# A decoder layer on one core: the first group of columns of the input projection, seven products of halves replaced by eight blocks summed in PSUM

## The chip, the cores and the metric

The kernel runs on one core of one Trainium2 chip. A core has a matrix engine (TensorE, in the profile PE for its matmuls and PEld for its weight loads), a vector engine (VectorE, DVE), a scalar engine (ScalarE, ACT), a general engine (GpSimd, POOL) and a queue that issues transfers (SyncE, SP). TensorE writes to PSUM, which has 8 banks of 512 numbers of 32 bits in each of 128 partitions; the other operands lie in SBUF. Each engine works through its own queue in order. The metric is the time of one execution on the device in microseconds (us); lower is better.

## The reference

The reference is one layer of a decoder on 2,048 tokens of 1,024 features, in 32-bit floats. Ahead of everything stands a normalised input and one wide projection:

```python
nx = rmsnorm(h, attn_norm_g[l])
proj = jnp.einsum('bsd,dp->bsp', nx, w_in[l])
gq, gk, gv, gr, glow, dq, dk_, dv_ = jnp.split(proj, split_at, axis=-1)
```

Then come two mixers side by side (a gated linear attention on gq, gk, gv, gr, glow and a dilated sliding-window attention on dq, dk, dv), an output projection, and an MLP with squared ReLU; a last normalisation ends it. The change touches only the start of the projection: the 512 columns of dv for the first 1,024 tokens.

## The kernel before, in words

**Precision.** TensorE multiplies in a reduced format, so each operand is split into a high and a low half (`split`: ACT copies the high half, L368; DVE subtracts it to get the low half, L369), and `mm3` issues three matmuls per product (L64, L65, L66).

**Seven products.** The projection is done for each group of columns and each half of the tokens. Within such a pair the tokens are cut in two (tiles 0 to 3 and 4 to 7 of 128 tokens each), the 1,024 features in two, and the columns in two, and the 2 x 2 blocks are multiplied by the scheme of Strassen and Winograd: seven products of halves instead of eight, numbered 1, 2, 5, 6, 3, 4, 7 in the order of `order`, with sums of token blocks (`first_half`, `sixth_sum`, `last_sums`) and of weight blocks (in `prep`) ahead, and sums of results (`rest` inside `product`) behind. A job is one (group, product). `prep(at)` splits the weights of a job into one of three buffers `combs` (L207 on ACT, L209 on DVE) and makes the sums of raw weights; `load_w` fetches a quarter of a group's weights (L190). `product(at, i)` issues the matmuls of tile i, 12 of 256 columns for a group 256 wide, and takes a PSUM bank for two tiles in the turn a, c, a, o; its `rest` moves the bank out (L325 to L342, ACT or DVE) and calls `finish`, which stores finished results (L277, L279 for dv). There are nine groups; dv is group 0, gr (2 x 264 columns) is group 1.

**Token parts.** `TF[j]` holds the split token operand of product j, high half and low half, each a slot of SBUF; `parts(j, i)` is tile i of it. For the first 1,024 tokens these parts are made inside group 0: `x_load` fetches a tile, `x_stat` squares and sums it (ACT L378, DVE L380, a power on POOL L381), `x_scale` scales it (DVE L385), `turned` transposes it on TensorE in 8 pieces into one bank c and one bank d (L393), `first_half` makes its parts, and `kept` copies tiles 0 to 3 back to SBUF for the later sums (ACT L404). 25 slots of one size hold all of this; a slot is given out at the first write, so product 7's high half gets the slot of tiles 6 and 7 (`xt`) when those have been read for the last time, and its low half takes one of the three weight buffers.

**Order.** All of group 0 of the first half stands in one section (from L496 on) where the order of TensorE, DVE, ACT and POOL is the order written in the program; only SP's is free. In the section the seven products are threaded through the arrival of the tiles: products 1 and 2 of tile 0, 1, 2, 3 between the transposes of tiles 0 to 5, then 5, 6 and 3, then 4 and 7. Everything behind the section is ordered by a planner that works with its own costs of instructions. The next jobs (group 1) follow in a loop in which job at is preceded by `prep(at + 2)`.

Of the kernel before, what the change touches and what calls it, by code (L numbers as in the profile page):

```python
# [38 lines left out]
def emit(tc, a, stop=99):  # L39
# [115 lines left out]


    misc = slot("misc")
    gB, gnB, w2b = misc[:, :D], misc[:, D:D + 512], misc[:17, D + 512:D + 768]
# [20 lines left out]
    TF = {j: [slot(f"tb{j}", FR) for _ in range(2 if j < 7 else 1)] for j in order}  # L179
    xt = slot("xt")  # L180
    TB = {j: [view(t, (4, 512)) for t in TF[j]] for j in order}
    xs = [t[:, D * q:D * q + D] for t in (xp, bp) for q in range(2)] + [c21[:, :D], last[:, :D]]
    xs += [xt[:, D * q:D * q + D] for q in range(2)]
# [12 lines left out]

    def prep(at, sums=True):

# [13 lines left out]
        if j == 2 and g:  # L212
            V.tensor_tensor(a21, a21, a22, op=OP.add)
        if j == 5 and sums:
            V.tensor_tensor(a21, a21, a11, op=OP.subtract)
            load_w(g + 1, 0, 0)
            V.tensor_tensor(a12, a12, a21, op=OP.subtract)
# [22 lines left out]
    def outputs(g):  # L240

        return (c11, (c12, c22)[g % 2], c21, (c22, c12)[g % 2])

# [38 lines left out]
    banks, held = [0], {}  # L282

    def product(at, i):

# [5 lines left out]
        if e == 0:  # L291
            held[j, i] = ps("acao"[banks[0] % 4])
            banks[0] += 1
        p = held[j, i - e]
# [72 lines left out]
    def split(hi, lo, src):  # L367
        A.activation(hi, src, AF.Copy)  # L368
        V.tensor_tensor(lo, src, hi.bitcast(F32), op=OP.subtract)  # L369
# [6 lines left out]
    def x_stat(t):  # L376
        ss = stat()
        A.activation(TF[4][0][:, :D], xs[t], AF.Square, accum_out=ss)  # L378
        r, X[t] = stat(), stat()
        V.tensor_scalar(r, ss, 1.0 / D, EPS, op0=OP.mult, op1=OP.add)  # L380
        G.tensor_tensor(X[t], r, mhalf, op=OP.pow)  # L381
# [24 lines left out]
    def first_half(t, pv):  # L406

        i = t % 4
        b11, b21 = [view(xs[i][:, 512 * q:], (4, 128)) for q in range(2)]
        if t < 4:  # L410
            split(*parts(1, i), pv[0])
            split(*parts(2, i), pv[1])
            return
        t1, t2 = [view(xs[t][:, 512 * q:], (4, 128)) for q in range(2)]
        V.tensor_tensor(t1, pv[0], b11, op=OP.subtract)
        V.tensor_tensor(t2, pv[1], t1, op=OP.subtract)
        split(*parts(5, i), t1)
        split(*parts(6, i), t2)
        split(*parts(3, i), pv[1])

    def sixth_sum(i):
        b21, t2 = [view(xs[k][:, 512:], (4, 128)) for k in (i, i + 4)]
        V.tensor_tensor(b21, b21, t2, op=OP.subtract)

    def sixth_part(i):
        split(*parts(4, i), view(xs[i][:, 512:], (4, 128)))

# [68 lines left out]
    with tc.manual_schedule(engines={nc.tensor.engine, nc.vector.engine, nc.scalar.engine, nc.gpsimd.engine}):  # L496
        x_load(0, xs[0])
        g1, one = c11[:1, :D], CX[:1, :128]
        A.dma_start(g1, a["attn_norm_g"])
# [3 lines left out]
        load_w(0, 0, 1)  # L503
        x_load(2, xs[2])
        x_load(3, xs[3])
        load_w(0, 1, 0)
        load_w(0, 1, 1)
# [10 lines left out]
        x_scale(0)  # L518
        prep(0)

        def turned(t):
            return transposed(xs[t], by=perm)

        x_stat(1)
        pv0 = turned(0)
        split(*parts(1, 0), pv0[0])
        x_scale(1)
        split(*parts(2, 0), pv0[1])
        rest = product(0, 0)
        prep(1)  # L530
        x_stat(2)
        rest()
        pv1 = turned(1)
        kept(0, pv0)
        x_scale(2)
        first_half(1, pv1)
        rest = product(1, 0)
        x_stat(3)
        pv2 = turned(2)
        rest()  # L540
        kept(1, pv1)
        a21, a22 = [raws[1][:, k, :, :256] for k in range(2)]
        V.tensor_tensor(a21, a21, a22, op=OP.add)
        x_scale(3)
        x_stat(4)
        first_half(2, pv2)
        rests = [product(at, 1) for at in (0, 1)]
        pv3 = turned(3)
        for rest in rests:
            rest()  # L550
        kept(2, pv2)
        x_scale(4)
        x_stat(5)
        first_half(3, pv3)
        rests = [product(at, 2) for at in (0, 1)]
        pv4 = turned(4)
        for rest in rests:
            rest()
        kept(3, pv3)
        x_scale(5)  # L560
        prep(2, sums=False)
        x_stat(6)
        first_half(4, pv4)
        for at in (0, 1):
            product(at, 3)()
        pv = turned(5)
        (a11, a12), (a21, a22) = [[raws[n][:, k, :, :256] for k in range(2)] for n in range(2)]
        V.tensor_tensor(a21, a21, a11, op=OP.subtract)
        load_w(1, 0, 0)
        V.tensor_tensor(a12, a12, a21, op=OP.subtract)  # L570
        prep(3)
        prep(4)
        x_stat(7)
        x_scale(6)
        product(2, 0)()
        product(3, 0)()
        first_half(5, pv)
        pv = turned(6)
        product(4, 0)()
        x_scale(7)  # L580
        product(2, 1)()
        first_half(6, pv)
        product(3, 1)()
        pv = turned(7)
        product(4, 1)()
        first_half(7, pv)
        for at in (2, 3, 4):
            product(at, 2)()
        TF[7].append(combs[2])
        TB[7].append(view(TF[7][1], (4, 512)))  # L590
        rests = [product(2, 3)]
        combs[2] = slot("wcomb", FR)
        prep(5)
        sixth_sum(0)
        sixth_sum(1)
        sixth_part(0)
        rests += [product(at, 3) for at in (3, 4)]
        sixth_part(1)
        sixth_sum(2)
        sixth_sum(3)  # L600
        sixth_part(2)
        rests[0]()
        sixth_part(3)
        rests[1]()
        third = rests[2]
        rests = [product(5, i) for i in range(4)]
        prep(6)
        for i in (2, 3, 0):
            last_sums(i)
        for i in range(4):  # L610
            if i == 1:
                last_sums(1)
            if i % 2:
                rests[i]()
            split(*parts(7, i), view(xs[i], (4, 128)))
            if i == 1:
                third()
        rests = [product(6, i) for i in range(4)]
        prep(7)
        for rest in rests:  # L620
            rest()
        prep(8)
    other, back = second_half(), []
    for at in range(7, len(jobs)):
# [905 lines left out]
```

## Time and profile before

| | |
|---|---|
| median of 3 runs | 2313.16 us (2312.07 to 2315.47) |
| the profiled execution's own time | 2312.57 us |
| its span, first to last instruction | 2310.8 us |
| mean granted TensorE clock | 0.995 |
| instructions | 34,890 |
| first matmul of a projection block | at 10.19 us |
| last matmul of group 0 of the first half | at 73.12 us |

Profile lines show a start in us from the span's beginning, a duration in us, the engine, the line of the kernel, the operation, what it writes and reads, and shapes; in brackets the idle time of the engine just before and what ended it. Matmuls overlap one another in the pipeline, so their cost is the distance from start to start and not the duration shown. In stretches of the span the columns are the stretch, its length, and for each engine the busy time with the number of instructions, then the granted TensorE clock as a share of full speed, the busy share of the DMA engines and what they moved in GB/s. A line can be that of a helper: `split` is L368 and L369 whoever calls it.

### The profile page before, as it was taken

The numbers are of one execution on the slowest core, as the hardware profiler recorded it, in microseconds if no ns is written. First come the engines' busy times: TensorE is split into PE (matmuls) and PEld (weight loads), VectorE is DVE, ScalarE is ACT, GpSimd is POOL, SyncE is SP. The second block draws the span as 40 slices with busy tenths as digits, with TensorE's granted clock in tenths as the row PEclk, the third lists the DMA queues.
The fourth block names the chain that finished last, engine by engine and source line by source line (L and its number), as shares of the span: only waits on it lengthen the run. The fifth ranks groups of instructions, "written<-read, shape, count | busy, mean of one in ns | idle before, by whom it ended". The sixth has DMA issues, their size and how long they took to land.

```text
span 2310.8 us, 34890 instructions
## 1 busy us (share of the span) xinstructions
PE 2282.6 (99%) x12652; PEld 1975.6 (85%) x12652; DVE 1550.3 (67%) x2863; ACT 1179.3 (51%) x2368; POOL 307.7 (13%) x394
## 2 busy tenths in 40 slices
PE   8999999999999999999999999999999999999998
PEld 7977998799999998888888888888888888888887
DVE  8887778766667676346877788777755346447444
ACT  5574546435877873235555566555543323225224
POOL 1120002025385672000000000000000100000002
PEclk9999999999999999999999999999999999999999
DMA  4457854786668864678644447444486477447553
GB/s 165 144 183 230 250 161 125 215 254 229 209 203 249 253 218 143 210 244 279 208 153 151 151 163 265 151 151 150 150 278 238 155 280 251 148 166 279 188 170 109
DMA packets 341805, 457.59 MB, mean 198 GB/s; under 512 B 18118, under 2 KB 214231, under 8 KB 336257
## 3 DMA queue, kind: packets, MB, share of 16 engines
q1 hardware_dynamic: 336878, 446.71, 59.3%
q10 hardware_dynamic: 4754, 8.66, 1.0%
q8 instruction: 99, 1.62, 0.3%
q14 instruction: 74, 0.60, 0.1%
HBM read 292.99 MB, written 167.02 MB: 199 GB/s over the span
## 4 chain that ended last, share of the span: by engine, by line
PE 51%; ACT 1%; DMA 0%; DVE 0%; issue 0%; DVEq 0%; ACTq 0%
PE ps_c L64 6%; PE ps_c L65 6%; PE ps_c L66 6%; PE ps_a L65 4%; PE ps_a L66 4%; PE ps_d L65 4%; PE ps_d L64 4%; PE ps_a L64 4%; PE ps_d L66 4%; PE ps_o L65 2%; PE ps_o L66 2%; PE ps_o L64 2%; DMA w1raw<-w_ff 0%; ACT scr L1355 0%; DVE hb L369 0%; ACT hb L368 0%
## 5 line engine op out<-in xcount | busy, mean ns | idle before, releaser
L369 DVE TENSOR_TENSOR ca<-ra,ca 128x1024 fp32r<-128x1024 f32 x112 | 138.0, 1233 | 161.6 <-ACT ca L368 161.6
L368 ACT ACTIVATE ca<-ra 128x1024 fp32r<-128x1024 f32 x112 | 118.0, 1053 | 221.3 <-PE ps_c L66 184.3
L368 ACT ACTIVATE w1comb<-w1raw 128x512 fp32r<-128x512 f32 x224 | 140.0, 627 | 153.7 <-PE ps_c L66 55.7
L1357 POOL TENSOR_TENSOR suma<-suma,gs 128x512 f32<-128x512 f32 x16 | 23.4, 1475 | 1393.7 <-ACT scr L1355 1393.7
L369 DVE TENSOR_TENSOR w1comb<-w1raw,w1comb 128x512 fp32r<-128x512 f32 x224 | 153.9, 689 | 51.8 <-ACT w1comb L368 51.7
L785 PE MATMUL ps_a<-v,pt 128*128 128x65 f32 x1200 | 178.2, 252 | 2.5 <-ACT pt L773 1.8
L785 PEld LDWEIGHTS ps_a<-v,pt 128*128 128x128 f32 x1200 | 175.1, 195 | 3.5 <-ACT pt L773 2.1
L757 ACT ACTIVATE pe<-pe,O 128x256 f32<-128x256 f32 (+1 forms) x384 | 156.6, 453 | 39.4 <-DVE O L756 36.1
L766 PE MATMUL ps_d<-ident,pe 128*128 128x128 f32 x600 | 159.9, 279 | 0.0
L756 DVE CUSTOM_DVE_ANT_0 pe<-ps_c,nb 128x256 f32<-128x256 f32 (+1 forms) x384 | 126.9, 361 | 39.6 <-PE ps_d L766 18.4
L207 ACT ACTIVATE wcomb<-wraw 128x512 fp32r<-128x512 f32 (+2 forms) x126 | 97.2, 773 | 88.7 <-PE ps_o L65 22.6
L368 ACT ACTIVATE cb<-rb 128x1024 fp32r<-128x1024 f32 x56 | 59.4, 1060 | 159.3 <-PE ps_o L65 98.8
L66 PE MATMUL ps_c<-cb,ca 128*128 128x512 f32 x336 | 130.7, 389 | 0.0
L66 PE MATMUL ps_c<-hb,w1comb 128*128 128x512 f32 x336 | 130.7, 389 | 0.0
L65 PE MATMUL ps_c<-cb,ca 128*128 128x512 f32 x336 | 130.7, 389 | 0.0
L64 PE MATMUL ps_c<-hb,w1comb 128*128 128x512 f32 x336 | 130.7, 389 | 0.0
L65 PE MATMUL ps_c<-hb,w1comb 128*128 128x512 f32 x336 | 130.7, 389 | 0.0
L64 PE MATMUL ps_c<-cb,ca 128*128 128x512 f32 x336 | 130.7, 389 | 0.0
L766 PEld LDWEIGHTS ps_d<-ident,pe 128*128 128x128 f32 x600 | 110.1, 187 | 0.1
L369 DVE TENSOR_TENSOR cb<-rb,cb 128x1024 fp32r<-128x1024 f32 x56 | 68.3, 1222 | 62.0 <-ACT cb L368 62.0
L1219 ACT ACTIVATE acc<-acc 128x512 f32<-128x512 f32 x128 | 79.6, 631 | 51.5 <-DVE acc L1239 35.8
L64 PE MATMUL ps_a<-wo,mT 128*128 128x512 f32 x256 | 101.3, 396 | 0.0
(419 smaller groups left out, 7038.9 us busy)
## 6 DMA issues: line engine op xcount, KB each, us to landing
ra<-actD SPq DMA_DIRECT2D x56, 1024.0 KB, 6.9
actD<-acc SPq DMA_DIRECT2D x192, 256.0 KB, 2.3
rb<-w_ff SPq DMA_DIRECT2D x72, 512.0 KB, 4.8
w1raw<-w_ff SPq DMA_DIRECT2D x32, 1024.0 KB, 6.2
k<-kD SPq DMA_DIRECT2D x16, 1024.0 KB, 7.9
rb<-hTD SPq DMA_DIRECT2D x13, 1024.0 KB, 7.1
wraw<-w_in SPq DMA_DIRECT2D x48, 256.0 KB, 3.7
cmb<-boD SPq DMA_DIRECT2D x16, 528.0 KB, 7.0
```

The lines of the kernel that those rows point to most:

```text
L64: T.matmul(out, sh, mh, start=first, stop=False)
L65: T.matmul(out, sl, mh, start=False, stop=False)
L66: T.matmul(out, sh, ml, start=False, stop=last)
L207: A.activation(hi, src, AF.Copy, scale=sc)
L368: A.activation(hi, src, AF.Copy)
L369: V.tensor_tensor(lo, src, hi.bitcast(F32), op=OP.subtract)
L756: V.tensor_tensor_reduce(p, s, bias, scale=1.0, scalar=BIG, op0=OP.add, op1=OP.min, accum_out=nm)
L757: A.activation(p, p, AF.Exp, bias=nm, scale=-1.0)
L766: T.transpose(pb[:, i * 128:i * 128 + 128], src, ident)
L785: T.matmul(self.b.opsum[:, n % 4], self.pt[:, i * 128:i * 128 + 128], self.b.v[:, blk, cols], start=first, stop=last)
L1219: A.activation(v, v, AF.Relu)
L1357: G.tensor_tensor(C[0], C[0], gF[:, :512], op=OP.mult)
```

## The change

Group 0 of the first half is no longer computed by seven products but block by block: for each half of the columns n, each half of the features k and each tile t, `block(n, k, t)` multiplies the tile's own split block by the weights' own split block, and the two values of k are summed in PSUM (32 blocks of 12 matmuls for 28). The weights need four plain splits (`prep_block`, into the three `combs` and the low half's slot of product 7, which is now given out at the start) and no sums; `taken(n, t)` copies a finished bank of two tiles out on ACT and stores it. The results of group 0 get their own places, the fourth of them CX. `first_half` of tiles 4 to 7 now makes the parts of the tile's own two blocks (kept for the time being in the places of products 4 and 3); the sums of tokens for products 5, 6, 4 and 7 are made in the same section, as are their parts, but later (`sum_parts`, `sixth_sum`, `last_sums`), since only group 1 reads them. The last tile is transposed when 14 of the 32 blocks have been issued. The third weight load moves ahead of the load of tile 3, the four loads of group 1's weights are issued together, and the first turn of the PSUM banks is c instead of a.

```diff
--- before.py
+++ after.py
     combs = [slot("wcomb", FR) for _ in range(3)]
     TF = {j: [slot(f"tb{j}", FR) for _ in range(2 if j < 7 else 1)] for j in order}
     xt = slot("xt")
+    TF[7].append(slot("wcomb", FR))
     TB = {j: [view(t, (4, 512)) for t in TF[j]] for j in order}
-    xs = [t[:, D * q:D * q + D] for t in (xp, bp) for q in range(2)] + [c21[:, :D], last[:, :D]]
+    xs = [t[:, D * q:D * q + D] for t in (xp, bp) for q in range(2)] + [c22[:, :D], last[:, :D]]
     xs += [xt[:, D * q:D * q + D] for q in range(2)]
...
@@ -239,6 +241,8 @@
 
     def outputs(g):
 
+        if g == 0:
+            return c11, c12, c21, CX
         return (c11, (c12, c22)[g % 2], c21, (c22, c12)[g % 2])
 
     def finish(g, n, k, i):
@@ -281,6 +285,36 @@
 
     banks, held = [0], {}
 
+    def bank():
+        banks[0] += 1
+        return ps("acao"[banks[0] % 4])
+
+    first_w = [[combs[1], TF[7][1]], [combs[0], combs[2]]]
+
+    def prep_block(n, k):
+
+        w = view(first_w[n][k], (2, 4, 256))
+        split(w[:, 0], w[:, 1], raws[n][:, k, :, :256])
+
+    def block(n, k, t):
+
+        i, e = t % 4, t % 2
+        if k == e == 0:
+            held["first", n, t] = bank()
+        q = held["first", n, t - e][:, 256 * e:256 * e + 256]
+        B = TB[((1, 2), (4, 3))[t // 4][k]]
+        W = view(first_w[n][k], (2, 4, 256))
+        tk = slice(i * 128, i * 128 + 128)
+        for c in range(4):
+            mm3(q, B[0][:, c, tk], B[1][:, c, tk], W[:, 0, c], W[:, 1, c], k == c == 0, k == 1 and c == 3)
+
+    def taken(n, t):
+
+        i = t % 4
+        A.activation(outputs(0)[2 * n + t // 4][:, 256 * i:256 * i + 512], held["first", n, t], AF.Copy)
+        for m in (i, i + 1):
+            finish(0, n, t // 4, m)
+
...
     def product(at, i):
 
 
@@ -289,8 +323,7 @@
         two = w == 256
         e = i % 2 if two else 0
         if e == 0:
-            held[j, i] = ps("acao"[banks[0] % 4])
-            banks[0] += 1
+            held[j, i] = bank()
...
     def x_stat(t):
         ss = stat()
-        A.activation(TF[4][0][:, :D], xs[t], AF.Square, accum_out=ss)
+        A.activation(CX[:, :D], xs[t], AF.Square, accum_out=ss)
         r, X[t] = stat(), stat()
         V.tensor_scalar(r, ss, 1.0 / D, EPS, op0=OP.mult, op1=OP.add)
         G.tensor_tensor(X[t], r, mhalf, op=OP.pow)
...
     def first_half(t, pv):
 
         i = t % 4
-        b11, b21 = [view(xs[i][:, 512 * q:], (4, 128)) for q in range(2)]
         if t < 4:
             split(*parts(1, i), pv[0])
             split(*parts(2, i), pv[1])
             return
         t1, t2 = [view(xs[t][:, 512 * q:], (4, 128)) for q in range(2)]
-        V.tensor_tensor(t1, pv[0], b11, op=OP.subtract)
+        split(*parts(4, i), pv[0])
+        split(*parts(3, i), pv[1])
+        V.tensor_tensor(t1, pv[0], view(xs[i], (4, 128)), op=OP.subtract)
         V.tensor_tensor(t2, pv[1], t1, op=OP.subtract)
-        split(*parts(5, i), t1)
-        split(*parts(6, i), t2)
-        split(*parts(3, i), pv[1])
+
+    def sum_parts(i):
+        for q in range(2):
+            split(*parts(5 + q, i), view(xs[i + 4][:, 512 * q:], (4, 128)))
 
     def sixth_sum(i):
         b21, t2 = [view(xs[k][:, 512:], (4, 128)) for k in (i, i + 4)]
         V.tensor_tensor(b21, b21, t2, op=OP.subtract)
-
-    def sixth_part(i):
-        split(*parts(4, i), view(xs[i][:, 512:], (4, 128)))
 
     def last_sums(i):
         b11, t2 = view(xs[i], (4, 128)), view(xs[i + 4][:, 512:], (4, 128))
...
         x_load(0, xs[0])
-        g1, one = c11[:1, :D], CX[:1, :128]
+        g1, one = c11[:1, :D], c12[:1, :128]
         A.dma_start(g1, a["attn_norm_g"])
         V.memset(one, 1.0)
         load_w(0, 0, 0)
         x_load(1, xs[1])
         load_w(0, 0, 1)
         x_load(2, xs[2])
+        load_w(0, 1, 0)
         x_load(3, xs[3])
-        load_w(0, 1, 0)
         load_w(0, 1, 1)
         for t in range(4, 8):
             x_load(t, xs[t])
@@ -516,110 +548,98 @@
             T.matmul(p, one, g1[:, 512 * q:512 * q + 512], start=True, stop=True)
             V.tensor_copy(gB[:, 512 * q:512 * q + 512], p)
         x_scale(0)
-        prep(0)
+        prep_block(0, 0)
 
         def turned(t):
             return transposed(xs[t], by=perm)
 
+        def both(n, t):
+            for k in range(2):
+                block(n, k, t)
+
         x_stat(1)
-        pv0 = turned(0)
-        split(*parts(1, 0), pv0[0])
+        pv = turned(0)
+        split(*parts(1, 0), pv[0])
         x_scale(1)
-        split(*parts(2, 0), pv0[1])
-        rest = product(0, 0)
-        prep(1)
+        split(*parts(2, 0), pv[1])
+        block(0, 0, 0)
+        prep_block(0, 1)
         x_stat(2)
-        rest()
-        pv1 = turned(1)
-        kept(0, pv0)
+        prep_block(1, 0)
+        kept(0, pv)
+        pv = turned(1)
+        block(0, 1, 0)
         x_scale(2)
-        first_half(1, pv1)
-        rest = product(1, 0)
+        first_half(1, pv)
+        block(1, 0, 0)
         x_stat(3)
-        pv2 = turned(2)
-        rest()
-        kept(1, pv1)
-        a21, a22 = [raws[1][:, k, :, :256] for k in range(2)]
-        V.tensor_tensor(a21, a21, a22, op=OP.add)
+        kept(1, pv)
+        pv = turned(2)
+        both(0, 1)
         x_scale(3)
+        first_half(2, pv)
+        prep_block(1, 1)
         x_stat(4)
-        first_half(2, pv2)
-        rests = [product(at, 1) for at in (0, 1)]
-        pv3 = turned(3)
-        for rest in rests:
-            rest()
-        kept(2, pv2)
+        kept(2, pv)
+        pv = turned(3)
+        block(1, 1, 0)
+        taken(0, 0)
         x_scale(4)
+        first_half(3, pv)
+        both(1, 1)
         x_stat(5)
-        first_half(3, pv3)
-        rests = [product(at, 2) for at in (0, 1)]
-        pv4 = turned(4)
-        for rest in rests:
-            rest()
-        kept(3, pv3)
+        kept(3, pv)
+        for n in range(2):
+            for k in range(2):
+                load_w(1, n, k)
+        pv = turned(4)
+        both(0, 2)
         x_scale(5)
-        prep(2, sums=False)
         x_stat(6)
-        first_half(4, pv4)
-        for at in (0, 1):
-            product(at, 3)()
+        first_half(4, pv)
+        taken(1, 0)
         pv = turned(5)
-        (a11, a12), (a21, a22) = [[raws[n][:, k, :, :256] for k in range(2)] for n in range(2)]
-        V.tensor_tensor(a21, a21, a11, op=OP.subtract)
-        load_w(1, 0, 0)
-        V.tensor_tensor(a12, a12, a21, op=OP.subtract)
-        prep(3)
-        prep(4)
+        both(0, 3)
+        x_scale(6)
         x_stat(7)
-        x_scale(6)
-        product(2, 0)()
-        product(3, 0)()
         first_half(5, pv)
         pv = turned(6)
-        product(4, 0)()
+        both(0, 4)
         x_scale(7)
-        product(2, 1)()
+        taken(0, 2)
         first_half(6, pv)
-        product(3, 1)()
         pv = turned(7)
-        product(4, 1)()
+        sum_parts(0)
+        both(0, 5)
         first_half(7, pv)
-        for at in (2, 3, 4):
-            product(at, 2)()
-        TF[7].append(combs[2])
-        TB[7].append(view(TF[7][1], (4, 512)))
-        rests = [product(2, 3)]
-        combs[2] = slot("wcomb", FR)
-        prep(5)
-        sixth_sum(0)
-        sixth_sum(1)
-        sixth_part(0)
-        rests += [product(at, 3) for at in (3, 4)]
-        sixth_part(1)
-        sixth_sum(2)
-        sixth_sum(3)
-        sixth_part(2)
-        rests[0]()
-        sixth_part(3)
-        rests[1]()
-        third = rests[2]
-        rests = [product(5, i) for i in range(4)]
-        prep(6)
-        for i in (2, 3, 0):
+        both(0, 6)
+        sum_parts(1)
+        taken(0, 4)
+        sum_parts(2)
+        sum_parts(3)
+        both(0, 7)
+        for i in (2, 3, 1, 0):
+            sixth_sum(i)
             last_sums(i)
-        for i in range(4):
-            if i == 1:
-                last_sums(1)
-            if i % 2:
-                rests[i]()
+        taken(0, 6)
+        both(1, 4)
+        prep(7)
+        both(1, 5)
+        for i in range(2):
+            split(*parts(4, i), view(xs[i][:, 512:], (4, 128)))
             split(*parts(7, i), view(xs[i], (4, 128)))
-            if i == 1:
-                third()
-        rests = [product(6, i) for i in range(4)]
-        prep(7)
-        for rest in rests:
-            rest()
+        taken(1, 4)
+        both(1, 6)
+        split(*parts(4, 2), view(xs[2][:, 512:], (4, 128)))
+        split(*parts(7, 2), view(xs[2], (4, 128)))
+        both(1, 7)
+        taken(1, 6)
+        split(*parts(4, 3), view(xs[3][:, 512:], (4, 128)))
+        split(*parts(7, 3), view(xs[3], (4, 128)))
+        both(1, 2)
+        both(1, 3)
         prep(8)
+        taken(1, 2)
```

More of the change, by code (lines that the diff above doesn't have):

```diff
@@ L195, in comb, with prep @@
         return [t[:, q, :, :w] for q in range(2)]
-    def prep(at, sums=True):
+    def prep(at):
         if at >= len(jobs):
@@ L213, in prep @@
             V.tensor_tensor(a21, a21, a22, op=OP.add)
-        if j == 5 and sums:
+        if j == 5:
             V.tensor_tensor(a21, a21, a11, op=OP.subtract)
```

## The prediction

> **What bounds the kernel now.** I read the page first: the busy shares and the slices.
>
> ```profile
> PE 2282.6 (99%) x12652; PEld 1975.6 (85%) x12652; DVE 1550.3 (67%) x2863; ACT 1179.3 (51%) x2368; POOL 307.7 (13%) x394
> ...
> PE   8999999999999999999999999999999999999998
> ...
> PEclk9999999999999999999999999999999999999999
> ```
>
> TensorE is busy for 99% of the span. So work taken off another engine is worth something only where TensorE stands still, and work added to TensorE costs its full price where it does not. Where it stands still is seen in stretches of the span (busy time and instruction count for PE, PEld, DVE, ACT, POOL, then granted clock, DMA share, GB/s).
>
> ```profile
> 15.00:73.00 58.00, 49.79 (x374) 48.28 (x373) 52.63 (x74) 32.54 (x55) 4.62 (x5) 0.91 0.38 121
> 73.00:115.00 42.00, 42.00 (x348) 42.00 (x347) 36.46 (x57) 26.36 (x63) 7.21 (x8) 1.00 0.49 139
> 115.00:825.00 710.00, 707.80 (x5071) 648.97 (x5069) 520.08 (x1392) 435.68 (x1079) 222.34 (x294) 1.00 0.68 212
> 825.00:900.00 75.00, 70.55 (x536) 66.24 (x535) 62.09 (x179) 49.48 (x133) 47.30 (x61) 0.95 0.65 209
> 900.00:2250.00 1350.00, 1348.99 (x6067) 1119.29 (x6067) 843.52 (x1116) 599.52 (x955) 11.53 (x8) 1.00 0.59 198
> ```
>
> The first row is the stage that the change rewrites. TensorE idles 8.2 us there and its clock is 0.91; DVE, busy 52.6 of 58.0 us, is the fuller engine. From 73 to 115 us TensorE has no gap, and in the 2,135 us from 115 to 2250 it idles 7.7 us, 4.5 of them in one stretch. So whatever TensorE gains before 73 us moves everything behind it forward. TensorE's waits in the stage name the stalls (total, times, longest):
>
> ```profile
> PE ps_c L64 <- ACT wcomb L207: 2.6, 1, 2.6
> PE ps_a L64 <- ACT tb L368: 2.6, 2, 2.4
> PE ps_c L393 <- DVE xt L385: 1.5, 1, 1.5
> PE ps_c L66 <- DVE wcomb L209: 0.8, 1, 0.8
> ```
>
> These are split weights, split parts of tokens and a scaled tile: all come late out of the two queues that DVE and ACT work through in order. The timeline of TensorE gives the pace:
>
> ```profile
> 14.99 0.40 PE L64 MATMUL ps_c<-wcomb,tb 128*128 128x256 f32 x1
> ...
> 20.29 0.60 PE L393 MATMUL ps_c<-perm,bp 128*128 128x128 f32 x4
> ...
> 21.08 0.37 PE L64 MATMUL ps_a<-wcomb,tb 128*128 128x256 f32 x1
> ...
> 22.59 0.28 PE L64 MATMUL ps_o<-wcomb,tb 128*128 128x256 f32 x1
> ...
> 24.04 0.60 PE L393 MATMUL ps_c<-perm,acc 128*128 128x128 f32 x4
> ...
> 36.84 0.41 PE L65 MATMUL ps_c<-wcomb,tb 128*128 128x256 f32 x1
> 37.05 0.41 PE L66 MATMUL ps_c<-wcomb,tb 128*128 128x256 f32 x1
> ...
> 69.19 0.41 PE L64 MATMUL ps_a<-wcomb,tb 128*128 128x256 f32 x1
> 69.40 0.41 PE L65 MATMUL ps_a<-wcomb 128*128 128x256 f32 x1
> ...
> 71.69 0.29 PE L64 MATMUL ps_a<-wcomb,tb 128*128 128x264 f32 x1
> ...
> 73.24 0.28 PE L66 MATMUL ps_a<-wcomb,tb 128*128 128x264 f32 x1
> ```
>
> Twelve matmuls of 256 columns (one tile, one product) take 1.45 us, from 22.59 to 24.04. Eight transposes with twelve such matmuls take 2.30 (20.29 to 22.59), so the transposes are 0.85. After the two long stalls a matmul starts only every 0.21 us (36.84 to 37.05, 69.19 to 69.40), where it is 0.12 at full pace: a stall of 2.4 us costs about 1.4 us more behind it. The two matmuls of the second group that lie ahead of 73.24 are worth 0.25, so the second group in effect begins at 73.0.
>
> **The change, part by part.**
>
> *TensorE.* Group 0 of the first half had 7 products of 4 tiles, 28 blocks of 12 matmuls; it gets 2 x 2 x 8 = 32. That is 4 more: 4 x 1.45 = 5.8 us, with nothing beside it to hide under. The transposes stay 64.
>
> *DVE and ACT.* Costs per instruction, as start to start where the queue is full:
>
> ```profile
> 10.86 1.28 DVE L385 SCALAR_TENSOR_TENSOR xp<-xp,stats,misc 128x1024 f32<-128x1024 f32 x1
> 12.06 0.68 DVE L369 TENSOR_TENSOR tb<-ps_d,tb 128x512 fp32r<-128x512 f32 x1
> 12.67 1.22 DVE L209 TENSOR_TENSOR wcomb<-wraw,wcomb 128x1024 fp32r<-128x1024 f32 x1
> ...
> 33.95 1.22 DVE L209 TENSOR_TENSOR wcomb<-wraw,wcomb 128x1024 fp32r<-128x1024 f32 x1
> 35.20 1.22 DVE L219 TENSOR_TENSOR wraw<-wraw 128x1024 f32<-128x1024 f32 x1
> 36.34 1.22 DVE L209 TENSOR_TENSOR wcomb<-wraw,wcomb 128x1024 fp32r<-128x1024 f32 x1
> ```
>
> ```profile
> 10.89 1.05 ACT L207 ACTIVATE wcomb<-wraw 128x1024 fp32r<-128x1024 f32 x1
> 11.84 1.05 ACT L378 ACTIVATE tb<-bp 128x1024 fp32r<-128x1024 f32 x1
> ...
> 12.87 0.59 ACT L404 ACTIVATE xp<-ps_c 128x512 f32<-128x512 f32 x1
> 13.35 0.59 ACT L404 ACTIVATE xp<-ps_d 128x512 f32<-128x512 f32 x1
> ...
> 20.71 0.60 ACT L404 ACTIVATE bp<-ps_c 128x512 f32<-128x512 f32 x1 [0.30 <-DVE tb L369]
> ```
>
> On DVE 1024 elements take 1.15 (33.95 to 36.34, two of them with the small gaps between 2.39, so 1.2 at the most), a scaling 1.2 and 512 elements 0.61; on ACT 0.95 and 0.48. DVE loses 3 of 7 weight splits and 4 sums of raw weights (7 x 1.15 = 8.1) and the 14 additions of group 0's evictions (14 x 0.61 = 8.5): 16.6 us of its 52.6. ACT loses 3 weight splits (2.9) and has 8 evictions for 6 (+1.0). The 28 splits of token parts, 16 sums of tokens, 8 scalings and 8 squares stay. DVE comes to about 36 us and TensorE becomes the fuller engine.
>
> *The end of the stage.* Up to 15.0 us nothing differs: the first block needs what the first product needed. From there 31 blocks and 6 transposed tiles remain: 31 x 1.45 + 6 x 0.85 = 50.1, so group 0 ends at 65.1 if TensorE never waits, against 73.0: a gain of 7.9, which I round to 8.0. The same sum for the order before, 27 blocks and 6 tiles, is 44.3 of the 58.0 us: 13.7 us are idle time, slow pace and restarts. They go, and 5.8 come.
>
> *Does TensorE never wait?* I followed the three queues by hand in the new order, with these durations. The third weight block is split on ACT at 12.87 and ready from DVE at 15.1; TensorE wants it at 16.5. Tile 2 is scaled at 16.7, wanted at 17.95. Tile 1's parts: 17.9, wanted at 18.8. The fourth weight block: 22.2, wanted at 22.6. Tile 4 scaled: 24.2, wanted at 26.9. Later margins are 2.5 us and grow. The smallest is 0.4, so I allow 0 to 1.5 us of waiting and take 0, since even a late block delays by its lateness alone. ACT's copy of a tile out of PSUM waits for DVE's low halves out of the same bank (20.71, 0.30 behind L369); that is in these times.
>
> *The power on POOL* that stands ahead of every scaling:
>
> ```profile
> 14.02 0.55 POOL L381 TENSOR_TENSOR stats<-stats,pair 128x1 f32<-128x1 f32 x1 [3.20 <-DVE stats L380]
> 17.23 1.46 POOL L381 TENSOR_TENSOR stats<-stats,pair 128x1 f32<-128x1 f32 x1 [2.66 <-DVE stats L380]
> ```
>
> It takes 0.55 and once 1.46, beside a DVE sum of two SBUF operands. In the new order the third weight block's low half stands at that place, so tile 2's power gets 1.46 in my times; it uses 0.4 of a margin of 1.6. The Trainium skill (SBUF — State Buffer, "Who interferes with whom") says that a VectorE instruction with two SBUF inputs holds off a GpSimd one that reads SBUF until it is done; the 1.46 agrees, and by it every power could be 0.9 late, which the scalings' margins (1.2 at the least) cover.
>
> *Loads.* Two transfers swap places (the third weight block goes ahead of tile 3), and the second group's four weight loads are issued together.
>
> ```profile
> 4.55 1.33 SPq L190 DMA_DIRECT2D wraw<-w_in  x2
> ...
> wraw<-w_in SPq DMA_DIRECT2D x4, 512.0 KB, 6.4
> ```
>
> The two last weight loads were issued from 4.55 and took 6.4: 11 us, one place earlier now, for 12.87. Tile 3 comes a transfer later; its square stands at 15.8. Bound: 0 to 1 us; I take 0. The second group's loads wait on SP behind two stores of the first eviction (ACT, 22.9) and land before 35; the split that needs them stands at 48.
>
> *Behind the stage.* Splits for products 4 and 7 and the second weight split move behind block matmuls. The second split must wait for the last block (65.1) and is done at 67.4; the product that reads it starts after 48 matmuls, at 71. The token parts of product 7 still need the buffer of tiles 6 and 7, which made the 2.4 us stall, but over 10 us of block matmuls and the whole of products 1 to 4 of the second group now lie ahead of their use. Stores: 16 and 4, as before. The rotation of PSUM banks begins one place on for all later groups; the trace does not show its price. TensorE idles 2.2 us from 115 to 825, so it is bounded by -2.2 (all of that gone) and +2.2 (as much again), and I take 0.
>
> The sum against the profiled execution: 2312.6 - 8.0 = 2304.6. The median of the runs is 0.6 above that execution: 2305.
>
> **The rivals.**
>
> *The new order starves TensorE at the start* (chance 0.12). If one of the thin margins (0.4 to 1.4) breaks by a late load, TensorE stands 2.4 us and then runs at the slow pace: 2.4 + 1.4 = 3.8 of the 8.0 are lost, 2309. For it: four weight splits and four tiles still crowd into the first 25 us of DVE. Against: the walk above, and DMA needs to be over 1.8 us late. The Trainium skill (TensorE: Matmul & The Clock Gate, "Part 1") has the clock fall after an idle window of about 3.4 us; here 2.4 to 2.6 us were enough, so the trace decides. By the page alone this rival would cost 2.4, not 3.8.
>
> *The planner gives it back* (0.14). Only this stage has its order written out; everything behind it is ordered by the planner, which now starts from another time and another bank. TensorE's 7.7 us of idle time from 115 to 2250 (and the slow clock of 0.95 in the one bad stretch, 3.7 us) show how little it loses today; a second stretch like the one from 825 to 900 would cost 4.5 + 3.7 = 8.2, and the time would be 2313. For it: nothing holds the old order. Against: the groups repeat, and a shift of all the work does not change who waits for whom.
>
> *ACT stands at the evictions, and the time rises* (0.12). Each of the 8 evictions waits in ACT's queue for the second tile of its pair; the splits behind it are then late, and TensorE waits for eviction, high half and low half, 0.48 + 0.6 + 0.7 = 1.8 us. Eight times that is 14.4: +6.4 in all, 2319.5. It decides from five evictions on. Against: after each, the split behind it is wanted 5 us later at the nearest (the third: eviction 34.6, parts ready at 37, wanted at 42).
>
> **How the numbers follow.** The forecast, 2305, has 0.62, with its own range 2303 to 2308 (8.0 with the bounds above: 1.5 of waits, 1.0 of loads, 2.2 either way of banks, not all at once). About 0.2%, 4.6 us, is what a measurement tells from no change. Faster by more than that: the forecast's 0.62, and 0.06 from a milder starving; within it 0.20; slower 0.12. The range 2301 to 2314 leaves out the slower rival and a little below, no more than 2 in 10.
>
> **What will show it.** The first matmul of 264 columns near 65 instead of 71.7, the clock in the stage from 15 us at 1.0, no wait of TensorE over 1 us there, DVE near 36 us busy up to that point, and later stretches as busy as now. Wrong would be: a TensorE wait for split weights or parts in the first 30 us; ACT ending TensorE's idle time behind an eviction; or a gain of 8 at 66 us that is gone at 900.

## The result and the profile after

The changed kernel takes 2305.73 us (median of 6 runs, 2303.79 to 2306.24), against 2312.68 us for the kernel before in the same comparison (6 runs, 2312.07 to 2315.47). The ratio is 0.9965, with a 95% interval of 0.9952 to 0.9978, which is 5.1 to 11.1 us. The forecast was 2305, a gain of 8.0.

The page of the profiled execution after the change (2305.64 us, span 2303.9), busy time and instruction counts:

```profile
PE 2281.4 (99%) x12700; PEld 1976.1 (86%) x12700; DVE 1533.8 (67%) x2846; ACT 1181.8 (51%) x2371; POOL 307.4 (13%) x394
```

TensorE is busy 1.2 us less than before, in a span that is 6.9 us shorter. So the gain is not work that left TensorE (it issues 48 matmuls more) but time in which it stood or ran slowly.

Stretches of the kernel after, with the columns of the prediction's table (busy time and count for PE, PEld, DVE, ACT, POOL, then granted clock, DMA share, GB/s). The later stretches are shifted by 8 us, so that they hold the work of 115 to 825 and of 825 to 900 before:

```profile
15.00:65.00 50.00, 49.39 (x414) 49.01 (x414) 38.53 (x59) 30.34 (x55) 2.91 (x6) 1.00 0.51 167
107.00:817.00 710.00, 707.59 (x5065) 649.82 (x5065) 520.59 (x1389) 436.35 (x1077) 222.28 (x294) 1.00 0.68 211
817.00:892.00 75.00, 68.56 (x531) 64.01 (x531) 60.80 (x179) 49.26 (x133) 46.91 (x61) 0.98 0.64 204
```

In the stage that was rewritten TensorE now idles 0.6 us instead of 8.2, and its clock is 1.00 instead of 0.91. The row from 107 us is like the one before; in the last one TensorE idles 6.4 us for 4.5, at a clock of 0.98 for 0.95. TensorE's waits up to 73 us (total, times, longest):

```profile
PE ps_a L548 <- DMA acc<-attn_norm_g: 2.3, 1, 2.3
PE ps_c L426 <- DVE xp L418: 1.9, 1, 1.9
PE ps_a L66 <- DVE wcomb L402: 0.4, 1, 0.4
PE ps_c L426 <- DVE bp L418: 0.2, 1, 0.2
```

The first two lie ahead of the first block. Of the stalls of 2.6, 2.4 and 1.5 us nothing is left. The timeline of TensorE shows where the 0.4 lies, which is the last wait in time, and where the stage begins and ends:

```profile
9.77 0.58 PE L64 MATMUL ps_c<-wcomb,tb 128*128 128x256 f32 x1
...
22.08 0.38 PE L66 MATMUL ps_a<-wcomb,tb 128*128 128x256 f32 x1 [0.39 <-DVE wcomb L402]
...
64.29 0.29 PE L64 MATMUL ps_c<-wcomb,tb 128*128 128x264 f32 x1
```

The wait at 22.08 is for the low half of the fourth weight block, the margin that the prediction had as its smallest. The second group begins at 64.3 (before: in effect 73.0).

The first block does not start at the same time in every execution (9.77 here, 10.19 before), because the first loads land at other times. So the stage is best measured from its first matmul to the first of the second group: 73.0 - 10.19 = 62.8 us before and 64.29 - 9.77 = 54.5 after.

### The profile page after: what moved, and what is told of

Its sections match the earlier page's. It is cut to its first block, busy times and chain, and to the rows that moved or that the text cites. A ratio compares the mean times of both kernels' runs of the same rounds, so it can differ in the third digit from the quotient of the medians.

```text
span 2303.9 us, 34945 instructions
## 1 busy us (share of the span) xinstructions
PE 2281.4 (99%) x12700; PEld 1976.1 (86%) x12700; DVE 1533.8 (67%) x2846; ACT 1181.8 (51%) x2371; POOL 307.4 (13%) x394
## 4 chain that ended last, share of the span: by engine, by line
PE 95%; DMA 1%; POOL 1%; DVE 1%; ACT 1%; issue 1%; DVEq 0%; ACTq 0%; POOLq 0%; SPq 0%
PE ps_a L65 10%; PE ps_a L66 10%; PE ps_a L64 10%; PE ps_c L64 8%; PE ps_c L66 8%; PE ps_c L65 8%; PE ps_d L65 4%; PE ps_d L64 4%; PE ps_d L66 4%; PE ps_a L805 4%; PE ps_o L66 4%; PE ps_o L64 4%; PE ps_o L65 4%; PE ps_d L786 3%; PE ps_c L764 2%; PE ps_c L766 2%
## 5 line engine op out<-in xcount | busy, mean ns | idle before, releaser
L401 ACT ACTIVATE w1comb<-w1raw 128x512 fp32r<-128x512 f32 x224 | 140.0, 627 | 154.6 <-PE ps_c L66 54.5
L209 ACT ACTIVATE wcomb<-wraw 128x512 fp32r<-128x512 f32 (+2 forms) x119 | 90.1, 758 | 97.8 <-PE ps_a L65 28.4
L402 DVE TENSOR_TENSOR cb<-rb,cb 128x1024 fp32r<-128x1024 f32 x56 | 68.3, 1222 | 64.3 <-ACT cb L401 64.3
```

Source lines behind the costliest of these rows:

```text
L209: A.activation(hi, src, AF.Copy, scale=sc)
```

## The experiments

All are edits of the changed kernel unless something else is said. "The stage" is that stretch, from the first matmul of 256 columns to the first of 264.

**Four blocks more.** The last four blocks of TensorE's work are issued twice, so TensorE gets the same amount of work again that the change added.

```diff
-        both(1, 2)
-        both(1, 3)
+        for _ in range(2):
+            both(1, 2)
+            both(1, 3)
```

> The changed kernel with the last four blocks of its first group issued twice (48 more matmuls of 256 columns; the result is the same). My theory, that TensorE alone sets the end of this stage and everything behind it moves with it: four blocks at 1.45 us are 5.8 us, so 2305.7 + 5.8 = 2311.5, and the first matmul of 264 columns at 64.3 + 5.8 = 70.1. The rival, that the stage ends when another engine is done (the weight split or the stores of the first group): 0 to 2 us, 2306 to 2307.5.

The time is 2313.51 us (2310.66 to 2314.36), ratio to the kernel before 0.9999 (0.9990 to 1.0009): the gain is gone. That is 2.0 more than expected; the kernel before was itself 1.6 slower in this comparison than in the one above (2314.31 against 2312.68). In the timeline:

```profile
10.48 0.58 PE L64 MATMUL ps_c<-wcomb,tb 128*128 128x256 f32 x1
...
70.75 0.28 PE L64 MATMUL ps_a<-wcomb,tb 128*128 128x264 f32 x1
```

The stage is 60.27 us, 5.75 more than 54.52: 48 matmuls at 0.12. The profiled execution, 2312.28, is 6.6 longer than that of the changed kernel, 0.7 of it from a later start. Work of TensorE in this stage has its full price in the stage, and the change paid 5.8 of it.

**DVE's work put back.** The new order, with idle work on DVE at about the places where the seven products had their splits, sums and additions: 7 operations of 1024 elements and 14 of 512. The result is unchanged.

```diff
+        def fill(n, times=1):
+            for _ in range(times):
+                V.tensor_tensor(gB[:, :n], gB[:, :n], gB[:, :n], op=OP.max)
...
         x_scale(5)
+        fill(1024)
         x_stat(6)
         first_half(4, pv)
         taken(1, 0)
+        fill(512)
+        fill(1024, 3)
```

> The changed kernel with the DVE work that the change took away put back as idle work of the same size: 7 operations of 1024 and 14 of 512 elements, spread over the section as the old sums and splits were (each takes the maximum of a row of factors with itself, so the result is the same). Theory, that the gain comes from DVE no longer holding TensorE up: TensorE waits again for scaled tiles and parts, 5 to 8 us of waits and slow clock in the stage, 2311 to 2314. The rival, that the gain comes from the order (blocks that need only a tile's own parts, so that TensorE has work in hand whatever DVE does): 0 to 2 us, 2306 to 2308.

The time is 2311.15 us (2308.56 to 2311.9), ratio 0.9986 (0.9976 to 0.9995), at the lower end of what the theory gave. The profiled execution is the fastest of the ten, 2308.56. TensorE's timeline in it:

```profile
9.45 0.58 PE L64 MATMUL ps_c<-wcomb,tb 128*128 128x256 f32 x1
...
37.85 0.66 PE L426 MATMUL ps_c<-perm,xt 128*128 128x128 f32 x4 [3.36 <-DVE stats L413]
...
38.90 0.28 PE L65 MATMUL ps_a<-wcomb,tb 128*128 128x256 f32 x1
39.02 0.28 PE L66 MATMUL ps_a<-wcomb,tb 128*128 128x256 f32 x1
...
68.46 0.29 PE L64 MATMUL ps_c<-wcomb,tb 128*128 128x264 f32 x1
```

The stage is 59.0 us, 4.5 more than in the changed kernel and still 3.8 less than before the change, with TensorE's four blocks more in it. So the relief of DVE is not the whole gain. And after a stall of 3.36 us the matmuls go on at 0.12 (38.90 to 39.02): no slow pace in this execution, although the prediction put 1.4 us behind a stall of 2.4. The other nine executions were 1.4 to 3.3 us longer, eight of them at a mean clock of 0.996 or 0.997 against 0.998 here, so slow pace may have followed their stalls; none of them has a profile.

**Seven products without the sums.** The order before the change, with its seven products, but group 0's raw weight sums and the additions of its evictions left out (so the columns of this group are not the reference's). DVE is relieved, TensorE's work is as before.

```diff
-        if j == 6:
+        if j == 6 and g:
             V.tensor_tensor(a21, a22, a21, op=OP.subtract)
...
+            if g == 0 and j in (2, 6, 3, 7):
+                A.activation({2: i11, 6: ix, 3: i12, 7: ix}[j], q, AF.Copy)
...
-        V.tensor_tensor(a21, a21, a22, op=OP.add)
...
-        V.tensor_tensor(a21, a21, a11, op=OP.subtract)
         load_w(1, 0, 0)
-        V.tensor_tensor(a12, a12, a21, op=OP.subtract)
```

> The kernel before, seven products in the old order, but in the first group of columns of the first half the four sums of raw weights and the sums of results are left out (a bank is moved out by one ACT copy instead), so its dv columns are not the reference's; about 13 us of DVE work go. Theory (DVE's load made the stalls): the stalls shrink, and since seven products need 44.3 us of TensorE from 15 us on, the stage ends between 60 and 65 instead of 73: 2300 to 2305. The rival (the stalls belong to the order of the seven products, whose parts are ready only when all tiles are in): the stage ends at 69 or later, 2309 or more.

The time is 2306.61 us (2305.47 to 2310.98), ratio 0.9968 (0.9957 to 0.9979). The two longest of TensorE's waits from 10 us on, and the ends of the stage:

```profile
PE ps_c L64 <- ACT wcomb L207: 0.9, 1, 0.9
PE ps_c L66 <- DVE wcomb L209: 0.8, 1, 0.8
```

```profile
10.27 0.58 PE L64 MATMUL ps_a<-wcomb,tb 128*128 128x256 f32 x1
...
65.80 0.29 PE L64 MATMUL ps_a<-wcomb,tb 128*128 128x264 f32 x1
```

The stage is 55.5 us: 7.3 less than before, without the four blocks. The same two splits are still waited for: the 2.6 has become 0.9, the 0.8 is as before. Both the end at 65.8 and the time lie just above what the theory gave (60 to 65, 2300 to 2305), and far from the rival's (69, 2309).

These four stages can be set beside TensorE's own work, 28 or 32 blocks of 1.45 and 7 tiles of 0.85 (tile 0 lies ahead of the first block): 46.55 us before, 52.35 after. What TensorE loses beside it is 16.2 us before, 9.0 with DVE relieved alone, 6.7 with the order changed alone, and 2.2 with both. Each does a good part by itself, 7.2 and 9.5, and they share 2.7. The ratios of the times, which rest on all runs and not on one profile each, say about the same when the 5.8 of the four blocks is added where they are in: 7.4 for the relief, 9.0 for the order, 13.9 for both, each uncertain by 2 to 3 us. (The idle work is not bound to data as the real one was, so the 6.7 is what such a load costs, not exactly what the seven products would.)

**The loads in the old order.** Tile 3 is loaded ahead of the third weight block again.

```diff
-        load_w(0, 1, 0)
         x_load(3, xs[3])
+        load_w(0, 1, 0)
```

> The changed kernel with the two swapped loads back in their old order (tile 3 ahead of the third block of weights). Theory, with the bound of 0 to 1 us that I gave the swap: at most 1 us slower, 2305.5 to 2307, with a wait of TensorE or ACT for that block under 1 us. The rival, that the swap is what keeps TensorE supplied at the start: a stall over 2.4 us with the slow clock behind it, 2309 or more.

The time is 2304.59 us (2303.67 to 2306.29), ratio 0.9961 (0.9948 to 0.9974):

```profile
10.27 0.58 PE L64 MATMUL ps_c<-wcomb,tb 128*128 128x256 f32 x1
...
64.77 0.29 PE L64 MATMUL ps_c<-wcomb,tb 128*128 128x264 f32 x1
```

The stage is 54.5 us, as in the changed kernel. The swap of the loads is worth nothing that these runs can tell.

**Short stalls.** Idle work on DVE ahead of three scalings, to see what a stall costs behind itself.

```diff
+        fill(1024, 2)
+        fill(512)
         x_scale(5)
...
+        fill(1024, 2)
         x_scale(6)
...
+        fill(1024, 2)
         x_scale(7)
```

> The changed kernel with idle work on DVE (a maximum of a tile with itself; the result is unchanged) ahead of the scalings of tiles 5, 6 and 7, 3.0, 2.4 and 2.4 us of it, so that TensorE stands three times some 2 to 2.5 us ahead of the transposes of these tiles. Theory A, the step of the prediction: each stall of about 2.4 us is followed by some 1.4 us of slow pace, so three spells at half clock, and the second group begins at 64.3 + 7 + 4 = 75.5. Theory B, from the recorded clock of the kernels so far: the clock is set for whole spells of 3.4 us on a fixed grid (35.5 to 42.3 and 66.3 to 69.7 before the change, 33.9 to 37.3 with seven products without sums), and falls only where one spell of the grid holds more than about 2 us of idle time (14, 18 and 35% of the matmuls that fit into it had started; at 42% it did not fall). By B a stall of 2.2 to 2.5 us is followed by slow pace in about half of the places it can lie in, so none to two of the three here, each spell exactly 3.4 us or a multiple, and the second group begins near 72 to 74; which of the stalls it is can be told from the end of the slow pace at the start of the same run, 3.413 us a step.

Only two stalls came of it, 2.28 and 0.87 us (tile 5 had more margin than I had allowed for), so the ends that both theories gave, 75.5 and 72 to 74, were missed. One run took 2308.05 us. The timeline of TensorE, and then two spells of 3.41 us (the granted clock is the third column from the right):

```profile
9.72 0.58 PE L64 MATMUL ps_c<-wcomb,tb 128*128 128x256 f32 x1
...
36.14 0.66 PE L426 MATMUL ps_c<-perm,xt 128*128 128x128 f32 x4 [2.28 <-DVE stats L413]
...
37.52 0.41 PE L65 MATMUL ps_a<-wcomb,tb 128*128 128x256 f32 x1
37.73 0.41 PE L66 MATMUL ps_a<-wcomb,tb 128*128 128x256 f32 x1
...
69.34 0.29 PE L64 MATMUL ps_c<-wcomb,tb 128*128 128x264 f32 x1
```

```profile
33.45:36.87 3.42, 1.14 (x10) 0.94 (x9) 3.30 (x5) 0.63 (x2) 0.55 (x1) 0.99 0.27 69
36.87:40.28 3.41, 3.41 (x19) 3.41 (x18) 3.34 (x5) 2.19 (x4) 0.00 (x0) 0.51 0.50 169
```

The 2.28 us lie in one spell, in which TensorE is busy for 1.14, and the whole next spell runs at half clock, though TensorE is busy in all of it. From 40.28 us on the clock is full again, and behind the 0.87 us nothing happens. The stage is 59.6 us, 5.1 more than 54.5: 2.28 + 0.87 + half of 3.41 make 4.9.

**One long stall.**

```diff
+        fill(1024, 6)
         x_scale(6)
```

> The changed kernel with 7.2 us of idle work on DVE (result unchanged) ahead of the scaling of tile 6, so that TensorE stands once for about 6.5 us ahead of that tile's transposes. Theory A (cost follows the stall): slow pace behind it for longer than behind a stall of 2.4 us, 3 us lost and more. Theory B (a fixed grid of 3.4 us): at least one spell of the grid is idle for over 2.1 us, so the clock falls for certain; how long it stays low depends on the grid and is 3.4 or 6.8 us, so 1.7 to 3.4 us are lost in every case, and the low clock can begin while TensorE still stands.

TensorE stands for 5.08 us, and one run took 2310.77 us:

```profile
10.23 0.58 PE L64 MATMUL ps_c<-wcomb,tb 128*128 128x256 f32 x1
...
39.43 1.11 PE L426 MATMUL ps_c<-perm,xt 128*128 128x128 f32 x4 [5.08 <-DVE xt L418]
...
72.48 0.29 PE L64 MATMUL ps_c<-wcomb,tb 128*128 128x264 f32 x1
```

```profile
34.73:38.14 3.41, 0.00 (x0) 0.00 (x0) 3.25 (x4) 0.26 (x1) 0.00 (x0) 0.99 0.49 147
38.14:41.55 3.41, 2.12 (x10) 2.12 (x11) 3.38 (x6) 0.71 (x2) 0.55 (x1) 0.50 0.26 89
41.55:44.97 3.42, 3.42 (x18) 3.42 (x17) 3.40 (x5) 1.52 (x3) 0.00 (x0) 0.51 0.01 2
```

The clock falls behind the idle spell, stays low through a spell in which TensorE is busy for 2.12 us, and through the next, which is full. The two cost (2.12 + 3.42) / 2 = 2.8 us; with the stall 7.9, and the stage is 72.48 - 10.23 = 62.25, 7.75 more than 54.5.

**The banks' turn.** One PSUM bank is skipped behind group 0, so that all later groups use the banks as before the change.

```diff
         taken(1, 2)
+        banks[0] += 1
```

> The changed kernel with one PSUM bank skipped behind group 0, so that the second group begins with the same bank as before the change. If the turn of the banks costs the changed kernel something behind the stage (it gained 8.7 us up to the second group and 6.9 at the end), the time falls by up to 1.8 us, to about 2304, and the stretch from the second group to the first matmul of attention comes down from 477.2 to 476.6 as before the change; if the turn is worth nothing, the time is 2305.7 within 0.7 and that stretch lies anywhere from 475.1 to 477.3, as in the runs so far.

The time is 2305.6 us (2303.55 to 2308.3), ratio 0.9965 (0.9951 to 0.9979):

```profile
10.21 0.58 PE L64 MATMUL ps_c<-wcomb,tb 128*128 128x256 f32 x1
...
64.72 0.29 PE L64 MATMUL ps_a<-wcomb,tb 128*128 128x264 f32 x1
```

The stage is 54.5, the median as without the edit. In the profiled execution, the slowest of the five (2308.3), the stretch from the second group to the first matmul that reads qs in attention is 478.3 us, longer than the 477.2 of the changed kernel and outside the 475.1 to 477.3 that was expected. So nothing comes back with the old turn of the banks.

**The kernel before, once more.**

> The kernel before, unchanged, for a second profile. If the 1.8 us that the change lost again behind the second group come from scatter between executions, the stretches of this profile (second group to attention 476.6, attention 331.3, the rest up to the last projection 1417.4) differ from the first one by up to 1 us each; if they belong to the change, these stretches repeat within 0.3 us. The slow spells of the clock in the stage: theory A (a stall of 2.4 us costs 1.4 more) has them again behind both stalls with the same loss; theory B (a fixed grid of 3.4 us that does not start with the kernel) has them at other places, or one of them not at all, and the second group then begins up to 3.4 us earlier or later than at 73.0.

One run took 2312.26 us. Its stage ends in effect at 71.9 (72.17 less the two matmuls of the second group that lie ahead), and the second fence shows the spells at its first stalls, to be set beside those of the first profile of the same kernel, which stand in the last one:

```profile
9.32 0.58 PE L64 MATMUL ps_a<-wcomb,tb 128*128 128x256 f32 x1
...
72.17 0.28 PE L66 MATMUL ps_a<-wcomb,tb 128*128 128x264 f32 x1
```

```profile
30.96:34.37 3.41, 0.53 (x3) 0.33 (x3) 3.34 (x4) 2.18 (x3) 0.00 (x0) 0.98 0.63 190
34.37:37.79 3.42, 2.48 (x10) 2.18 (x10) 3.42 (x4) 0.97 (x2) 0.96 (x1) 0.50 0.72 204
37.79:41.20 3.41, 3.11 (x15) 3.14 (x16) 3.21 (x6) 1.75 (x3) 0.56 (x1) 0.52 0.51 158
```

```profile
32.07:35.48 3.41, 0.76 (x4) 0.56 (x5) 3.34 (x4) 2.42 (x3) 0.00 (x0) 1.00 0.70 211
35.48:38.89 3.41, 1.99 (x10) 1.69 (x9) 3.41 (x5) 0.74 (x2) 1.19 (x1) 0.51 0.70 188
38.89:42.31 3.42, 3.35 (x16) 3.38 (x17) 3.21 (x6) 1.75 (x3) 0.33 (x1) 0.50 0.47 153
...
62.85:66.26 3.41, 0.87 (x5) 0.67 (x6) 2.65 (x5) 1.12 (x2) 0.00 (x0) 1.00 0.55 159
66.26:69.67 3.41, 3.41 (x19) 3.41 (x18) 2.71 (x6) 3.32 (x6) 0.00 (x0) 0.50 0.71 198
```

The stage repeats: 62.6 us against 62.8, with the same stalls (2.4 and 2.6 us the longest) and three slow spells again (the third from 65.0 to 68.4). That they would come at other places (theory B's second half) was a miss: in both executions the grid stood alike against the kernel. From the second group, counted from where it in effect begins, to the first matmul that reads qs in attention 476.6 became 476.5, but from there to the first matmul with wo it took 331.3 and then 332.9. The clock accounts for about as much, half of 3.41 us: near the end of attention it fell for one spell of 3.41 us in the first profile (871.8 to 875.3) and for two in the second (870.6 to 877.4).

## Why the prediction was right, point by point

**The bound and the sum.** Right. The stage went from 62.7 (mean of the two profiles) to 54.5, a gain of 8.2 where the prediction, with its end at 65.1 less the start at 10.19, had 54.9 and 7.9. The 54.5 came out in the changed kernel, with the loads swapped back and with the banks turned back; with four blocks more it was 60.27 - 5.76 = 54.5 too.

**Four blocks, 5.8 us.** Measured at 5.75.

**DVE down by 16.6 us to about 36.** The row from 15 to 65 us shows 38.5. It holds 30 splits of 512 elements where the row before held 26, so the difference is four of them, 4 x 0.69 = 2.8; I had not counted that they now fall into this window. It cost nothing, since DVE is not the fuller engine any more after 22 us.

**The causes of the 13.7 us.** Here the prediction's reason was too narrow: it let DVE's relief carry the gain. The order alone, with the load put back, took 9.5 of the 16.2 us that TensorE loses from its first matmul on, and the relief alone 7.2 (9.0 and 7.4 by the ratios of the times). The walk through the queues was right because it followed the new order with the new load, not because DVE was lighter alone.

**The margins.** The one for the fourth weight block, 0.4, came out as a wait of 0.4. Tile 2's scaling, with 1.2 to spare in the walk, became one of 0.2, since TensorE came to it early. The later margins held. The start is even tighter than the walk had it. Full clock began some 3 us earlier in this profile (matmuls 0.12 apart from 11.9 us on, before from 15.2), and the stage did not become shorter by it: with the banks turned back full clock came only at 14.3, TensorE then did not wait, and the stage was 54.5 as well. In the changed kernel DVE's queue up to the fourth weight block sets the first 12.3 us, so an earlier full clock turns into waiting. That block's low half is the end of DVE's queue there:

```profile
20.81 1.21 DVE L402 TENSOR_TENSOR wcomb<-wraw,wcomb 128x1024 fp32r<-128x1024 f32 x1
```

The power on POOL took 1.56 (from 13.60 us) at the place for which 1.46 was assumed.

**"A stall of 2.4 us costs about 1.4 us more behind it."** Wrong as a rule, and this is the step that failed. The clock is set for whole spells of 3.41 us that follow a grid. 2.28 us inside one spell cost 1.7 more, 3.36 us across the border of two cost nothing, 0.87 nothing, 5.08 cost 2.8. Before the change the first stall, with the two shorter ones beside it, cost two slow spells, (1.99 + 3.35) / 2 = 2.7, and the second one 3.41 / 2 = 1.7. So 4.4 of the 13.7 us were slow clock, where the step would give 2.8. The sum did not suffer, since it took the 13.7 as a whole. The Trainium skill (TensorE: Matmul & The Clock Gate, "Part 1") says that the window of about 3.4 us is free-running; the spells of 3.41 us agree. It has the clock fall after an idle window, and here a window need not be idle: TensorE was busy in it for 0.53 to 1.14 us.

**Loads and banks taken at 0.** Each was taken back by an edit of its own, and the median moved by 1.1 us and by 0.1, within the scatter; the stage is 54.5 with and without.

**Behind the stage, taken at 0.** From the second group to the end of the span it is 2237.8 and 2238.6 us in the two profiles before, 2239.6 after, 2238.4 with the loads swapped back and 2241.8 with the banks turned back; over all ten profiles it is 2236.5 to 2241.8. So the 8.2 of the stage became 6.9 between the two profiles, and the median's 6.95, with an interval of 5.1 to 11.1, agrees with 8.2. Part of this scatter is the clock: between the stage and the end the profile with the shortest stretch (one long stall) has one spell of 3.41 us at half clock, the one with the longest (banks turned back) has four, and the others two or three. One place did change. At the start of attention TensorE waits for DVE, 0.6 us in both profiles before and in the seven products without sums, 1.1 to 1.8 in all profiles of the new order but the one with four blocks more. In the changed kernel and with the banks turned back a slow spell follows. The first line is from before, the other two from after:

```profile
536.06 0.37 PE L744 MATMUL ps_c<-k,qp 128*128 128x256 f32 x1 [0.63 <-DVE O L756]
```

```profile
526.64 0.38 PE L764 MATMUL ps_c<-k,qp 128*128 128x256 f32 x1 [1.74 <-DVE O L776]
```

```profile
527.18:530.59 3.41, 3.41 (x18) 3.41 (x17) 1.68 (x14) 2.81 (x10) 3.41 (x5) 0.50 0.96 290
```

That is 1.1 us of waiting and 1.7 of slow clock. Up to attention's first matmul the changed kernel had been 1.8 quicker than before (458.4 us behind the second group's start, before 460.2), and at the first matmul that reads qs it is 0.7 slower (477.2 against 476.6). Why DVE comes later there was not tried.

**The rivals.** Starving at the start: not seen, 0.6 us of waits instead of 3.8. ACT at the evictions: no wait of TensorE in the changed kernel's stage ends on ACT. The planner: the stretch from 817 to 892 us idles 6.4 us against 4.5, but at a clock of 0.98 against 0.95; no second stretch of that size appeared. The loss at the start of attention is a small case of what this rival said.

## What to carry to other kernels

Where an engine is busy 99% of the time, look at its first hundred microseconds by themselves: work can be added to it there and time still be gained, if the stalls that go are longer than the work that comes. Price the end of such a stage by the full engine's own work at full pace, walk the other queues once to see that it never waits, and measure the stage from its first matmul, since the start scatters by a microsecond. A test that gives back one cause at a time (the load without the order, the order without the load) shows how much each is worth, which the sum alone does not.

## What the runs showed of the hardware

Between its first full clock and the last 7 us of the span, TensorE's clock fell to half for spells of 3.41 us or two of them, never for another length, in all ten profiles. In this stage it fell behind each of the spells in which TensorE was busy for 0 to 1.14 us. With 1.66 and 1.80 us (the stall of 3.36 us across a border) it did not fall:

```profile
32.83:36.24 3.41, 1.66 (x14) 1.46 (x13) 3.34 (x3) 0.60 (x1) 0.00 (x0) 1.00 0.00 0
36.24:39.65 3.41, 1.80 (x16) 1.80 (x17) 3.32 (x6) 1.11 (x3) 0.55 (x1) 1.00 0.76 238
```

With 1.75, in the seven products without sums, it did:

```profile
30.42:33.83 3.41, 1.75 (x12) 1.34 (x12) 2.30 (x3) 3.41 (x6) 0.00 (x0) 1.00 0.38 105
33.83:37.25 3.42, 2.96 (x15) 2.70 (x14) 3.31 (x6) 0.95 (x4) 1.52 (x1) 0.51 0.82 255
```

Behind the stage 1.75 us in 19 matmuls and transposes (the banks turned back) was followed by a slow spell, and 1.94 in 9 (the loads in the old order) was not:

```profile
830.12:833.53 3.41, 1.75 (x19) 1.56 (x17) 3.15 (x14) 2.39 (x6) 3.26 (x5) 1.00 0.54 210
```

```profile
182.82:186.23 3.41, 1.94 (x9) 1.43 (x9) 2.34 (x4) 3.38 (x8) 0.00 (x0) 1.00 1.03 376
```

So the border lies near half of a spell by busy time, not sharply (1.66 did not, 1.67 in the changed kernel at 523.77 did), and the number of matmuls does not decide it; what does is open. In the stage the clock came back behind a slow spell with 2.96 us of work or more, and did not behind 1.99, 2.12 and 2.48. This does not hold everywhere: with the loads in the old order a slow spell with 3.42 us of work (862.08 to 865.50) was followed by a second one.
